# Grouped TensorE products in a two-layer hybrid encoder: chained units, fewer state copies, and attention values placed before the next transposes

## The chip, the cores and the metric

The kernel runs on one core of a Trainium2 chip. The metric is the time of one execution on the device in microseconds (us), as the median of several runs.

## What is computed

Two layers, each with three parallel branches on 256 tokens of width 1024, then a gated feed-forward block. All inputs and outputs are float32. Cut to what the change touches:

```python
for l in range(DEPTH):                      # DEPTH = 2
    h = _rmsnorm(x, norm1_g[l])
    # one projection h @ w_in[l], split into q, k, v, gate of the retention branch,
    # the low-rank inputs of attention, s5_u, and the three branch gates
    ...
def attend(blk):                            # attention branch, 8 heads, 256 keys
    sc = einsum('bhqd,bhkd->bhqk', qn, k_nope) + einsum('bhqd,bkd->bhqk', qr, k_rope)
    p = softmax(sc, axis=-1)
    return einsum('bhqk,bhkd->bhqd', p, v)
...
# S5 branch, both directions: 64 groups of 16 channels, a complex state of 64 each
bu = einsum('bsgc,gpc->bsgp', u_g, bb)      # re and im
x_t = abar * x_{t-1} + bu_t                 # associative scan over the 256 tokens
y = Re(einsum('bsgp,gcp->bsgc', x, c))      # + d * u, then gelu and a GLU
```

## The kernel before

**Main work.** Weights are streamed from HBM in tiles of 512 KB (`raw`). ScalarE rounds a tile to a high part (`wh`, L668), VectorE subtracts to get the low part (`wl`, L669), and TensorE makes three products for each block of 128 rows (`mm3`, L673 to L675: high by high, high by low, low by high) into the PSUM banks of pool `pw`. These products of 256 columns are called main products below. They run in both layers from start to end.

**S5 work.** The S5 branch is a generator (`s5`) that the main work advances in small steps (`tick`), so that its instructions are traced between the main products. The 256 tokens are cut into 32 blocks of 8. For each of 16 steps `qq` (four groups of 16 channels at a time) `s5_wt` builds weights on VectorE (L523 to L531), transposes them on TensorE (L536, four in a bank of `p5`) and copies them out (L538). Then four products, one for each group, go to four strips of 32 columns of the array (`tile_position`, L452, tile `p`, called state products). After every second step the bank is copied (L459), transposed (L462) and written by ScalarE in eight copies of 64 by 128 elements into the state tile `SS` (L467, L468). In layer 1 the built weights come back from HBM (`wtd`). After a scan over the blocks on VectorE (L480 to L483), `s5_out` makes for each step `q` a set of small kernels: two directions by four strips (L584, tile `p`), whose bank goes to HBM as `kd` and comes back in another layout as `wt`; `s5_emit` then accumulates the outputs of two steps (L629, tile `pa`, called output products): for each step the products with the forward states, with the backward states (both read `wy`) and with `wt`. A float32 product is two instructions on TensorE, a transpose is one.

**Attention.** `attend` (L1110 on) goes over eight heads: `score` (four products, L1134 and L1135, then maximum, exponent and scaling on VectorE and ScalarE), `turn` (four transposes, L1153, and one copy, L1156), and the product with the values (L1170, two for each head, two heads in one bank). Between them `more` pulls steps of the first branch's main products.

**What sets the order.** The program is traced and a scheduler then orders each engine's instructions by priority, by its own estimate of when operands and buffers are ready; every engine works through its list in order. PSUM has eight banks: three in `pw`, three in `pa` (scores, transposes, attention values, output products), two in `p5` (everything else of S5). Buffers of a tag rotate: a new tile waits until the readers of an old one are done. Two banks of `p5` mean that a second set of L536 transposes waits while a bank of transposed states is still read by the copies L467 and L468. SBUF buffers named `at` hold the scores and their transposes, two before the change.

## Time and profile before

| what | us |
|---|---|
| median of three runs | 1431.8 (1431.16 to 1436.98) |
| the profiled execution | 1425.45 |
| its span | 1423.5 |
| TensorE (PE) busy | 1334.4, 94% |
| VectorE (DVE) busy | 1042.3, 73% |
| ScalarE (ACT) busy | 807.0, 57% |

Busy times of PE are of pipelined instructions, whose shown durations overlap: a main product lasts 0.28 us in the records, and the next begins 0.12 us after it. What an instruction costs on PE is therefore read from start to start. The chain of work that ended last lies on PE for 68% of the span. S5 states are built between about 65 and 222 us in layer 0 and between 820 and 887 us in layer 1; S5 outputs between 298 and 443 us and between 976 and 1128 us, in the same stretches as attention.

### The profile page before, as it was taken

The page shows a single profiled execution, that of the slowest core. Times are in us where ns is not written, and L with a number is a line of the kernel's source. Part 1 is how long each engine was busy: PE and PEld are TensorE (multiplying, and loading weights), DVE is VectorE, ACT ScalarE, POOL GpSimd, SP SyncE. Part 2 cuts the span into 40 slices and gives each one's busy share as a digit, 9 for nine tenths or more (in the row PEclk, how much of TensorE's full clock was granted, in tenths as well). Part 3 has the DMA queues.
Part 4 walks back from the last instruction along what each step waited for, and adds up shares of the span by engine and source line. Part 5 has one row for each costly group of instructions (what it writes and reads, how often), then busy time and mean ns, then how long its engine had stood idle before and what let it go on. Part 6 is the DMA issues. An engine that isn't in the chain of part 4 may idle for free.

```text
span 1423.5 us, 27613 instructions
## 1 busy us (share of the span) xinstructions
PE 1334.4 (94%) x11102; PEld 1234.2 (87%) x11102; DVE 1042.3 (73%) x1910; ACT 807.0 (57%) x1339; POOL 4.5 (0%) x33
## 2 busy tenths in 40 slices
PE   7899998888999999999999999788999999999997
PEld 5866878867888999999999868778988899999997
DVE  7977867877687679988668547877768657777754
ACT  3656576974654455545446677786564344544442
POOL 0000000000000000000000000000000000000000
PEclk9999999999999999999999999999999999999999
DMA  8944233646786699766679784365687667666662
GB/s 218 250 146 118 69 104 99 182 137 152 211 219 194 201 211 260 210 199 197 188 229 273 239 267 131 99 193 156 157 247 188 193 200 204 181 185 187 179 179 79
DMA packets 433891, 260.84 MB, mean 183 GB/s; under 512 B 61714, under 2 KB 413284, under 8 KB 433764
## 3 DMA queue, kind: packets, MB, share of 16 engines
q1 hardware_dynamic: 433764, 259.09, 64.3%
q8 instruction: 87, 1.43, 0.4%
q14 instruction: 40, 0.33, 0.1%
HBM read 231.53 MB, written 27.53 MB: 182 GB/s over the span
## 4 chain that ended last, share of the span: by engine, by line
PE 68%; ACT 13%; DMA 8%; DVE 6%; issue 3%; SPq 1%; DVEq 0%; ACTq 0%
PE pw L673 17%; PE pw L674 17%; PE pw L675 17%; DMA wt<-kd 3%; ACT wh L668 3%; PE pw L713 2%; PE pw L714 2%; PE pw L715 2%; DVE wl L669 2%; DMA kd<-ev 2%; ACT s L497 2%; PE p L536 2%; PE p L452 2%; DMA raw<-in_w_in 1%; SPq L121 1%
## 5 line engine op out<-in xcount | busy, mean ns | idle before, releaser
L673 PE MATMUL pw<-s,wh 128*128 128x256 f32 x2472 | 714.6, 290 | 16.6 <-ACT wh L668 13.8
L675 PE MATMUL pw<-s,wl 128*128 128x256 f32 x2472 | 703.5, 285 | 8.4 <-DVE wl L669 8.3
L674 PE MATMUL pw<-s,wh 128*128 128x256 f32 x2472 | 703.0, 285 | 0.2 <-DVE s L749 0.2
L668 ACT CAST wh<-raw 128x1024 fp32r<-128x1024 f32 (+4 forms) x394 | 381.0, 972 | 456.2 <-PE pw L674 290.7
L669 DVE TENSOR_TENSOR wl<-raw,wh 128x1024 fp32r<-128x1024 f32 (+4 forms) x394 | 443.1, 1128 | 206.8 <-ACT wh L668 205.4
L673 PEld LDWEIGHTS pw<-s,wh 128*128 128x128 f32 x2472 | 472.1, 191 | 34.1 <-ACT wh L668 16.6
L675 PEld LDWEIGHTS pw<-s,wl 128*128 128x128 f32 x2472 | 472.5, 191 | 15.5 <-DVE wl L669 11.2
L674 PEld LDWEIGHTS pw<-s,wh 128*128 128x128 f32 x2472 | 472.9, 191 | 6.6 <-issue 4.8
L713 PE MATMUL pw<-s,wh 128*128 128x256 f32 x256 | 71.9, 281 | 0.0
L714 PE MATMUL pw<-s,wh 128*128 128x256 f32 x256 | 71.9, 281 | 0.0
L715 PE MATMUL pw<-s,wl 128*128 128x256 f32 x256 | 71.9, 281 | 0.0
L569 DVE TENSOR_TENSOR wy<-s,s 128x512 f32<-128x512 f32 x64 | 42.3, 687 | 16.1 <-PE pa L629 10.3
L715 PEld LDWEIGHTS pw<-s,wl 128*128 128x128 f32 x256 | 48.2, 188 | 0.0
L714 PEld LDWEIGHTS pw<-s,wh 128*128 128x128 f32 x256 | 48.2, 188 | 0.0
L713 PEld LDWEIGHTS pw<-s,wh 128*128 128x128 f32 x256 | 48.2, 188 | 0.0
L536 PE MATMUL p<-ident,wy 128*128 128x128 f32 x256 | 36.7, 276 | 11.5 <-ACT s L468 11.1
L497 ACT COPY s<-s 64x256 f32<-64x256 f32 (+1 forms) x64 | 40.7, 636 | 5.2 <-DVE s L483 4.3
L536 PEld LDWEIGHTS p<-ident,wy 128*128 128x128 f32 x256 | 28.6, 140 | 16.6 <-ACT s L468 13.2
L570 DVE TENSOR_TENSOR tm<-s,s 128x512 f32<-128x512 f32 x64 | 43.0, 687 | 0.0
L571 DVE TENSOR_TENSOR wy<-wy,tm 128x512 f32<-128x512 f32 x64 | 42.7, 685 | 0.0
L748 ACT ACTIVATE s<-ev 128x512 fp32r<-128x512 f32 x46 | 29.1, 633 | 19.7 <-DVE ev L1350 12.1
L531 DVE TENSOR_TENSOR wy<-wy,tm 128x1024 f32<-128x1024 f32 x32 | 39.1, 1221 | 0.3
(284 smaller groups left out, 1549.7 us busy)
## 6 DMA issues: line engine op xcount, KB each, us to landing
raw<-in_w_in SPq DMA_DIRECT2D x122, 512.0 KB
raw<-in_ffn_w_gu SPq DMA_DIRECT2D x88, 512.0 KB
raw<-in_w_branch SPq DMA_DIRECT2D x48, 512.0 KB
raw<-in_s_w_glu SPq DMA_DIRECT2D x32, 512.0 KB
raw<-in_ffn_w_down SPq DMA_DIRECT2D x32, 512.0 KB
wt<-kd SPq DMA_DIRECT2D x64, 128.0 KB
raw<-in_w_out SPq DMA_DIRECT2D x16, 512.0 KB
wtd<-wt SPq DMA_DIRECT2D x16, 512.0 KB
```

Source lines behind the costliest of these rows:

```text
L497: A.copy(*todo.pop(0))
L536: T.transpose(ps[:, i * P:(i + 1) * P], W[i % 2][:, gp * 2 + i // 2].rearrange("p s c -> p (s c)"), self.ident)
L570: V.tensor_tensor(t2, tv(1), cv(C2), ALU.mult)
L571: V.tensor_tensor(y[:, :, js, :], y[:, :, js, :], t2, ALU.add)
L668: self.nc.scalar.copy(hi, src)
L669: self.nc.vector.tensor_tensor(lo, src, hi.bitcast(F32), ALU.subtract)
L673: T.matmul(ps, lh, rh, start=first, stop=False)
L674: T.matmul(ps, lh, rl, start=False, stop=False)
L675: T.matmul(ps, ll, rh, start=False, stop=last)
L713: T.matmul(o, wh[:, k, c], xh, start=(half == 0 and m == 0 and k == 0), stop=(k == 3), **f)
L714: T.matmul(o, wh[:, k, c], xl, start=False, stop=(k == 3), **f)
L715: T.matmul(o, wl[:, k, c], xh, start=False, stop=(k == 3), **f)
```

## The change

A context manager `unit` is added: it records an ordering edge between each two PE instructions that are traced in it, from one to the one before, so that the scheduler keeps their order among themselves. It is put around the state products, the transposes L462 and L536, the kernels L584, and the products and transposes of retention and attention. Within such groups the order is changed so that those that need the operand that is made last come first.

The eight copies into `SS` become four of 64 by 256 elements. Before, a copy read runs of 32 neighbours in PSUM and wrote each element 256 bytes from the last; now it writes runs of eight neighbours and reads PSUM at steps of 128 bytes.

In `s5_emit` the products with the states of both steps come first, and then those with `wt` of both. In `attend` the value product of a head is put off until the transposes of the next head, after both calls of `more`; `more` counts to 17 instead of 16; `at` gets a third buffer, and the buffers of the scan (`sc`) go from four to two.

```diff
+    @contextmanager
+    def unit(self):
+
+        traced = self.nc.cur_bb.bb.instructions
+        n = len(traced)
+        yield
+        last = None
+        for i in traced[n:]:
+            if i.engine != mybir.EngineType.PE:
+                continue
+            if last is not None:
+                self.tc.add_manual_dep(i, last.name, mybir.DependencyInfo(
+                    mybir.DependencyClass.NoSync, mybir.DependencyReason.DATA), reason="unit")
+            last = i
...
-            for g4 in range(4):
-                T.matmul(plv[g4 * 32:g4 * 32 + 32, :],
-                         UT[qq // 8][:, qq % 8, g4 * 32:g4 * 32 + 32],
-                         WT[:, g4].rearrange("p r x -> p (r x)"), start=True, stop=True, tile_position=(0, g4 * 32))
+            with self.unit():
+                for g4 in (2, 3, 0, 1):
+                    T.matmul(plv[g4 * 32:g4 * 32 + 32, :],
+                             UT[qq // 8][:, qq % 8, g4 * 32:g4 * 32 + 32],
+                             WT[:, g4].rearrange("p r x -> p (r x)"), start=True, stop=True,
+                             tile_position=(0, g4 * 32))
...
-            for i in range(4):
-                T.transpose(pt[:, i * P:(i + 1) * P], lq[:, i * P:(i + 1) * P], self.ident)
-            ptv = pt.rearrange("p (q r h n) -> p q r h n", q=2, r=2, h=4)
-            for q2 in range(2):
-                g0 = (qq - 1 + q2) * 4
-                for r in range(2):
-                    A.copy(SS[0:64, r, :, g0:g0 + 4].rearrange("p n h -> p h n"), ptv[0:64, q2, r])
-                    A.copy(SS[64:128, r, ::-1, g0:g0 + 4].rearrange("p n h -> p h n"), ptv[64:128, q2, r])
+            with self.unit():
+                for i in range(4):
+                    T.transpose(pt[:, i * P:(i + 1) * P], lq[:, i * P:(i + 1) * P], self.ident)
+            ptv = pt.rearrange("p (q r h n) -> p r n q h", q=2, r=2, h=4)
+            g0 = (qq - 1) * 4
+            for r in range(2):
+                o = lambda rows, step: SS[rows, r, ::step, g0:g0 + 8].rearrange("p n (q h) -> p n q h", q=2)
+                A.copy(o(slice(0, 64), 1), ptv[0:64, r])
+                A.copy(o(slice(64, 128), -1), ptv[64:128, r])
...
-            r1 = self.s(128, "sc", 4).rearrange("p (r g) -> p r g", r=2)
-            r2 = self.s(128, "sc", 4).rearrange("p (r g) -> p r g", r=2)
+            r1 = self.s(128, "sc", 2).rearrange("p (r g) -> p r g", r=2)
+            r2 = self.s(128, "sc", 2).rearrange("p (r g) -> p r g", r=2)
...
-            for d in range(2):
-                for g4 in range(4):
-                    gm = q * 4 + g4
-                    c0 = (q % 2) * 240 + (112 if d == 0 else 0)
-                    js = slice(0, 8) if d == 0 else slice(1, 9)
-                    T.matmul(pk[g4 * 32:g4 * 32 + 32, c0:c0 + 128],
-                             BB2[:, d, gm * 16:gm * 16 + 32],
-                             Y[d][:, g4, js, :].rearrange("p j c -> p (j c)"),
-                             start=(d == 0), stop=True, tile_position=(0, g4 * 32), skip_group_check=(d == 1))
+            with self.unit():
+                for d in (1, 0):
+                    for g4 in range(4):
+                        gm = q * 4 + g4
+                        c0 = (q % 2) * 240 + (112 if d == 0 else 0)
+                        js = slice(0, 8) if d == 0 else slice(1, 9)
+                        T.matmul(pk[g4 * 32:g4 * 32 + 32, c0:c0 + 128],
+                                 BB2[:, d, gm * 16:gm * 16 + 32],
+                                 Y[d][:, g4, js, :].rearrange("p j c -> p (j c)"),
+                                 start=(d == 1), stop=True, tile_position=(0, g4 * 32), skip_group_check=(d == 0))
...
-        for q_, Yq in pend:
-            oc = (q_ % 4) * 128
-            for k in range(3):
-                for g4 in range(4):
-                    gm = q_ * 4 + g4
-                    if k == 0:
-                        lhsT, rhs = Sf[:, gm, :], Yq[0][:, g4, 1:9, :].rearrange("p j c -> p (j c)")
-                    elif k == 1:
-                        lhsT, rhs = Sb[:, gm, :], Yq[1][:, g4, 0:8, :].rearrange("p j c -> p (j c)")
-                    else:
-                        lhsT, rhs = UT[:, q_, g4 * 32:g4 * 32 + 32], M[:, g4, q_ % 2, :]
-                    T.matmul(po[g4 * 32:g4 * 32 + 32, oc:oc + 128], lhsT, rhs, start=(k == 0), stop=(k == 2),
-                             tile_position=(0, g4 * 32))
+        for ks in ((0, 1), (2,)):
+            for q_, Yq in pend:
+                oc = (q_ % 4) * 128
+                for k in ks:
+                    for g4 in range(4):
+                        gm = q_ * 4 + g4
+                        if k == 0:
+                            lhsT, rhs = Sf[:, gm, :], Yq[0][:, g4, 1:9, :].rearrange("p j c -> p (j c)")
+                        elif k == 1:
+                            lhsT, rhs = Sb[:, gm, :], Yq[1][:, g4, 0:8, :].rearrange("p j c -> p (j c)")
+                        else:
+                            lhsT, rhs = UT[:, q_, g4 * 32:g4 * 32 + 32], M[:, g4, q_ % 2, :]
+                        T.matmul(po[g4 * 32:g4 * 32 + 32, oc:oc + 128], lhsT, rhs,
+                                 start=(k == 0 and q_ % 2 == 0), stop=(k == 2), tile_position=(0, g4 * 32),
+                                 skip_group_check=True)
...
-            while done[1] < done[0] * steps // 16:
+            while done[1] < done[0] * steps // 17:
...
-            for kt in range(2):
-                for t in range(2):
-                    T.transpose(pt[:, kt * S + t * P:kt * S + t * P + P], pe[:, t * S + kt * P:t * S + kt * P + P],
-                                self.ident)
+            with self.unit():
+                for t in (1, 0):
+                    for kt in range(2):
+                        T.transpose(pt[:, kt * S + t * P:kt * S + t * P + P],
+                                    pe[:, t * S + kt * P:t * S + kt * P + P], self.ident)
             pts = self.s(512, "at")
             A.copy(pts, pt)
             return pts
 
-        pe = score(0)
-        for hd in range(MH):
-            more()
-            pts = turn(pe)
-            if hd + 1 < MH:
-                pe = score(hd + 1)
-            more()
+        def value(hd, pts):
             if hd % 2 == 0:
-                po = self.bank(self.pa)
-            vv, hh = kvs[hd // 4][1], hd % 4
+                value.po = self.bank(self.pa)
+            po, vv, hh = value.po, kvs[hd // 4][1], hd % 4
             for kt in range(2):
                 T.matmul(po[:, (hd % 2) * S:(hd % 2 + 1) * S], vv[:, kt * 512 + hh * MV:kt * 512 + (hh + 1) * MV],
                          pts[:, kt * S:(kt + 1) * S], start=(kt == 0), stop=(kt == 1))
             if hd % 2 == 1:
                 self.put(y, hd - 1, 2, po)
+
+        pe, held = score(0), None
+        for hd in range(MH):
+            more()
+            more()
+            if held:
+                value(hd - 1, held)
+            held = turn(pe)
+            if hd + 1 < MH:
+                pe = score(hd + 1)
+        more()
+        value(MH - 1, held)
         run(work)
```

Indentation apart, the other hunks put `with self.unit():` around loops that stay as they were; the transposes of retention's `finish` also change their order as those of `turn` do. A line of before and its number after the change: L452 is L469, L536 is L556, L629 is L651, L673 to L675 are L696 to L698, L1134 and L1135 are L1161 and L1162, L1153 is L1181, L1170 is L1192.

How the instructions stand on PE in layer 0, where states are built, from the second set of L536 transposes of a step (weights of step `qq` = 2) on. Before:

```order
L536 MATMUL p_171_905<-ident,wy_892 128x128 x4
L452 MATMUL p_172_911<-wt_898,s_124_625 32x256 x2
L673 MATMUL pw_922<-s_34_212,wh_925 128x256
L674 MATMUL pw_922<-s_36_214,wh_925 128x256
L675 MATMUL pw_922<-s_34_212,wl_926 128x256
L673 MATMUL pw_922<-s_34_212,wh_925 128x256
L452 MATMUL p_172_911<-wt_898,s_124_625 32x256 x2
```

The same place after the change:

```order
L556 MATMUL p_171_901<-ident,wy_888 128x128 x4
L697 MATMUL pw_918<-s_35_213,wh_921 128x256
L698 MATMUL pw_918<-s_33_211,wl_922 128x256
L696 MATMUL pw_918<-s_34_212,wh_921 128x256
L697 MATMUL pw_918<-s_36_214,wh_921 128x256
L698 MATMUL pw_918<-s_34_212,wl_922 128x256
L696 MATMUL pw_918<-s_34_212,wh_921 128x256
L697 MATMUL pw_918<-s_36_214,wh_921 128x256
L698 MATMUL pw_918<-s_34_212,wl_922 128x256
L469 MATMUL p_172_907<-wt_894,s_124_625 32x256 x4
```

The two halves of a step's state products, with four main products between them, have become one group behind eight main products.

PE in layer 1, the first output products (`s5_emit`) of that layer. Before:

```order
L629 MATMUL pa_11463<-wy_11410,s_1706_10257 32x128 x4
L629 MATMUL pa_11463<-wy_11410,s_1707_10258 32x128 x4
L629 MATMUL pa_11463<-wt_11609,s_1574_9529 32x128 x4
L629 MATMUL pa_11463<-wy_11520,s_1706_10257 32x128 x4
L629 MATMUL pa_11463<-wy_11520,s_1707_10258 32x128 x4
L629 MATMUL pa_11463<-wt_11609,s_1574_9529 32x128 x4
L1170 MATMUL pa_11751<-at_11625,s_1881_11099 128x256 x2
```

The same place after the change:

```order
L651 MATMUL pa_11396<-wy_11346,s_1706_10193 32x128 x4
L651 MATMUL pa_11396<-wy_11346,s_1707_10194 32x128 x4
L651 MATMUL pa_11396<-wy_11430,s_1706_10193 32x128 x4
L651 MATMUL pa_11396<-wy_11430,s_1707_10194 32x128 x4
L651 MATMUL pa_11396<-wt_11541,s_1574_9497 32x128 x8
L696 MATMUL pw_11626<-s_1422_8677,wh_11689 128x256
```

The products with `wt`, which comes from HBM, stand eight products later for the first of the two steps.

PE in layer 0, attention, transposes of the second head and scores of the third. Before, where two sets of S5 transposes (L389) lie among the scores:

```order
L675 MATMUL pw_3133<-s_244_1292,wl_3184 128x256
L1153 MATMUL pa_3273<-ident,at_3082 128x128 x4
L1134 MATMUL pa_3280<-s_552_2897,s_486_2615 128x256
L389 MATMUL p_627_3256<-ident,s_624_3249 128x128 x4
L1135 MATMUL pa_3280<-kab_2182,s_488_2617 128x256
L1134 MATMUL pa_3280<-s_552_2897,s_486_2615 128x256
L389 MATMUL p_628_3264<-ident,s_624_3249 128x128 x4
L1135 MATMUL pa_3280<-kab_2182,s_488_2617 128x256
```

The same place after the change, with the values of the first head ahead:

```order
L698 MATMUL pw_3241<-s_34_212,wl_3245 128x256
L1192 MATMUL pa_3293<-at_3082,s_553_2866 128x256 x2
L1181 MATMUL pa_3296<-ident,at_3094 128x128 x4
L1161 MATMUL pa_3303<-s_552_2865,s_486_2583 128x256
L1162 MATMUL pa_3303<-kab_2154,s_488_2585 128x256
L1161 MATMUL pa_3303<-s_552_2865,s_486_2583 128x256
L1162 MATMUL pa_3303<-kab_2154,s_488_2585 128x256
L696 MATMUL pw_3241<-s_33_211,wh_3321 128x256
```

Values, transposes and scores stand in a row here. In the whole program that is so for two heads of sixteen (one before); value products stand directly ahead of a set of transposes seven times (twice before).

In the whole program the state products stand in 30 runs of two, 15 of four and one of eight before, and in 30 of four and one of eight after; the kernels L584 in 20 runs of four and 22 of eight before, and in 31 of eight, one of five and one of three after. PE has 10076 products and transposes both times, ACT 66 instructions fewer.

## Rows read from the trace of the kernel before

**Rows 1.** The page's first part: busy us, share of span, instructions, by engine.

```profile
PE 1334.4 (94%) x11102; PEld 1234.2 (87%) x11102; DVE 1042.3 (73%) x1910; ACT 807.0 (57%) x1339; POOL 4.5 (0%) x33
```

**Rows 2.** Stretches: length, busy PE, PEld, DVE, ACT, POOL, clock, DMA share, GB/s.

```profile
75.00:215.00 140.00, 128.58 (x858) 102.55 (x857) 105.50 (x202) 86.95 (x158) 0.54 (x4) 0.98 0.36 104
450.00:800.00 350.00, 347.77 (x2874) 343.95 (x2873) 281.13 (x423) 182.84 (x252) 0.17 (x1) 1.00 0.77 218
```

**Rows 3.** PE's timeline: start us, us; a half and a full group of state products.

```profile
130.77 0.28 PE L674 MATMUL pw<-s,wh 128*128 128x256 f32 x1
130.89 0.28 PE L675 MATMUL pw<-s,wl 128*128 128x256 f32 x1
131.10 0.63 PE L452 MATMUL p<-wt,s 128*32 128x256 f32 x4
...
131.88 0.28 PE L674 MATMUL pw<-s,wh 128*128 128x256 f32 x1
...
872.29 0.28 PE L675 MATMUL pw<-s,wl 128*128 128x256 f32 x1
872.49 0.64 PE L452 MATMUL p<-wt,s 128*32 128x256 f32 x8
...
873.28 0.28 PE L674 MATMUL pw<-s,wh 128*128 128x256 f32 x1
```

**Rows 4.** PE's timeline: a half and a full group of the kernels L584.

```profile
402.68 0.28 PE L675 MATMUL pw<-s,wl 128*128 128x256 f32 x1
402.90 0.43 PE L584 MATMUL p<-wy,t_bb 128*32 128x128 f32 x8
...
403.48 0.28 PE L674 MATMUL pw<-s,wh 128*128 128x256 f32 x1
...
1086.17 0.28 PE L675 MATMUL pw<-s,wl 128*128 128x256 f32 x1
1086.38 0.64 PE L584 MATMUL p<-wy,t_bb 128*32 128x128 f32 x16
...
1087.18 0.28 PE L674 MATMUL pw<-s,wh 128*128 128x256 f32 x1
```

**Rows 5.** PE's waits from 75 to 215 us: total us, times, longest us.

```profile
PE p L536 <- ACT s L468: 11.1, 7, 1.8
```

**Rows 6.** ACT's copies by form: busy us, mean ns, idle before.

```profile
L497 ACT COPY s<-s 64x256 f32<-64x256 f32 x48 | 31.3, 652 | 5.0 <-DVE s L483 4.3
L467 ACT COPY s<-p 64x128 f32<-64x128 f32 x64 | 24.2, 378 | 2.1 <-PE p L462 1.5
L373 ACT COPY s<-ev 64x256 f32<-64x256 f32 x8 | 3.2, 406 | 1.1 <-DMA ev<-pxd 1.1
```

**Rows 7.** A wait for the copies on PE's timeline, and the stretch behind it.

```profile
82.07 0.66 PE L536 MATMUL p<-ident,wy 128*128 128x128 f32 x4 [1.74 <-ACT s L468]
...
83.00:86.40 3.40, 3.40 (x16) 1.98 (x13) 1.92 (x3) 1.40 (x3) 0.00 (x0) 0.50 0.38 134
```

**Rows 8.** Waits for `wt` (300 to 450, 975 to 1130 us); 48 output products in the chain.

```profile
PE pa L629 <- DMA wt<-kd: 7.8, 14, 1.1
...
PE pa L629 <- DMA wt<-kd: 3.6, 5, 1.0
...
399.42 1.45 PE pa L629 x48
```

**Rows 9.** DVE's largest wait from 75 to 215 us.

```profile
DVE wl L669 <- ACT wh L668: 14.5, 14, 5.1
```

**Rows 10.** Attention: PE's wait for a bank (300 to 450 us); ACT's copy; ACT's cast.

```profile
PE pa L1134 <- ACT at L1156: 0.9, 1, 0.9
...
L1156 ACT COPY at<-pa 128x512 f32<-128x512 f32 x16 | 9.4, 588 | 3.0 <-PE pa L1153 2.9
...
L668 ACT CAST wh<-raw 128x1024 fp32r<-128x1024 f32 (+4 forms) x394 | 381.0, 972 | 456.2 <-PE pw L674 290.7 <-issue 86.8 <-PE pw L714 35.0
```

More of the change, by code (lines that the diff above doesn't have):

```diff
@@ L1 @@
 import math
+from contextlib import contextmanager
 import numpy as np
@@ L935, in score @@
             qh, kh = q[:, hd * S:(hd + 1) * S], k[:, hd * S:(hd + 1) * S]
-            for s_ in range(2):
-                T.matmul(ps[:, s_ * S:(s_ + 1) * S], kh[:, s_ * P:(s_ + 1) * P], qh, start=True, stop=True)
+            with self.unit():
+                for s_ in range(2):
+                    T.matmul(ps[:, s_ * S:(s_ + 1) * S], kh[:, s_ * P:(s_ + 1) * P], qh, start=True, stop=True)
             V.scalar_tensor_tensor(dec, ps, sc, dec, ALU.mult, ALU.mult)
@@ L942, in value @@
             py = self.bank(self.pa)
-            for tt in range(2):
-                for s_ in range(2):
-                    T.matmul(py[:, tt * S:(tt + 1) * S], dec[:, s_ * S + tt * P:s_ * S + tt * P + P],
-                             vt[s_][:, hd * RV:(hd + 1) * RV], start=(s_ == 0), stop=(s_ == 1))
+            with self.unit():
+                for tt in range(2):
+                    for s_ in range(2):
+                        T.matmul(py[:, tt * S:(tt + 1) * S], dec[:, s_ * S + tt * P:s_ * S + tt * P + P],
+                                 vt[s_][:, hd * RV:(hd + 1) * RV], start=(s_ == 0), stop=(s_ == 1))
             st = self.s(12, "gst", 2).rearrange("p (t x) -> p t x", t=2)
@@ L964, in finish @@
             ps = self.bank(self.pa)
-            for i in range(2):
-                for tt in range(2):
-                    T.transpose(ps[:, i * S + tt * P:i * S + tt * P + P],
-                                yn[:, tt * S + i * P:tt * S + i * P + P], self.ident)
+            with self.unit():
+                for tt in (1, 0):
+                    for i in range(2):
+                        T.transpose(ps[:, i * S + tt * P:i * S + tt * P + P],
+                                    yn[:, tt * S + i * P:tt * S + i * P + P], self.ident)
             for i in range(2):
```

20 lines of the change are left out of this document (11 added, 9 removed).

## The prediction

> **What bounds the kernel now.** I read the busy times first [rows 1]: TensorE is busy for 94% of the span, VectorE for 73%, ScalarE for 57%. So time can be saved in two ways only: PE needs less time for the same products, or PE waits less. Then the stretches [rows 2]. From 450 to 800 us, where main products alone run, PE is never late although VectorE is busy for 80% (281.1 of 350 us). From 75 to 215 us, where S5 states are built, PE is busy for 92% (128.6 of 140 us) and VectorE for 75%. The change acts in the second kind of stretch. Last, PE's timeline start to start, because busy times of pipelined products overlap: this shows what a group of strip products costs in its place.
>
> **State products, L452.** A half group (two products, four instructions) stands between two main products. From the main product ahead of it to the second one behind it are 0.99 us (130.89 to 131.88), and a full group of eight instructions takes the same 0.99 us (872.29 to 873.28) [rows 3]. Two strips cost as much as four: the time goes into the passes that the strips share, and into entering and leaving. Both stretches hold two main products, at 0.12 us each (130.77 to 130.89) [rows 3]. Two halves cost 2 x 0.99 = 1.98 us; one full group and the two main products that then stand elsewhere cost 0.99 + 0.24 = 1.23 us. Each joining saves 0.75 us, and the order shows 15 (30 runs of two become 15 of four): 11.2 us, nearly all in the stretch from 75 to 215 us.
>
> **Kernels, L584.** A half group takes 0.80 us (402.68 to 403.48), a full one 1.01 us (1086.17 to 1087.18) [rows 4]; here the strips are full anyway and only entering and leaving is saved. Joining saves 2 x 0.80 - 1.01 - 0.24 = 0.35 us. The order goes from 42 runs to 33: 9 x 0.35 = 3.2 us. The runs of output products go from 31 to 30, which I leave out. PE time saved: 14.4 us. It lies on the path as far as PE is the bound there.
>
> **Copies into the state tile.** In layer 0 PE waits seven times for them, 11.1 us in all, before the second set of L536 transposes [rows 5]: both banks of `p5` are taken, one by the transposed states until the eighth copy has read them. Eight copies at 0.38 us make 3.04 us [rows 6]. What one of the four new copies takes, no row shows. Lower end: 0.41 us, a copy of 64 by 256 without scattered access (L373). Upper end: 0.76 us, the old price for each element. The nearest row in shape is L497 with 0.65 us: it also writes runs of eight and reads at wide steps, but from SBUF [rows 6]. The source here is PSUM, so I take 0.53 us, midway between L373 and L497. Four copies make 2.12 us; each of the seven waits shrinks by 0.92 us, as ten main products or so still stand ahead of the waiting transposes: 6.4 us. The ends are 7 x (3.04 - 1.64) = 9.8 us and nothing. Layer 1's eight sets and layer 0's last relieve ScalarE alone, counted at nothing.
> [...]
>
> **The clock.** [...] I take 0.8 us; ends 0 and 3 us, for another such place.
>
> **Output products, L629.** PE waits 19 times for `wt` from HBM, 7.8 + 3.6 = 11.4 us [rows 8]. Up to four of these waits belong to one call of `s5_emit`, so 5 to 16 calls wait. Now the second step's products with the states, 16 instructions, come first: 48 take 1.45 us [rows 8], so 0.48 us of work moves ahead of the wait. I take seven calls: 3.4 us; ends 2.4 and 7.7 us. The DMAs behind it are the same and stand at the same places on SP's queue relative to the kernels that feed them.
>
> **Attention.** The value products now come after more main products, so their copy is ready; that can only help PE. Scores follow the transposes as before, in 10 heads instead of 12 without main products between them. PE waited for a bank there once, 0.9 us [rows 10]. I put the sum at nothing; ends a gain of 2 us and the loss of the fourth rival. `at` with three buffers and `sc` with two: each step of the scan needs the step before it, so two `sc` buffers hide nothing, and cost nothing.
>
> **What is given back.** With 11.2 + 6.4 + 0.8 = 18.4 us less, the stretch of 140 us would be 121.6 us long, and VectorE's 105.5 us there would be 87% of it, above the 80% that another stretch bears without waits [rows 2]. VectorE also waits 14.5 us for ScalarE's casts there [rows 9], and these waits don't vanish all. To come down to 80% the stretch needs 131.9 us, which gives 10.3 us back. I take 4 us, nearer to nothing, because the buffers for high and low parts let VectorE work ahead; ends 0 and 10.3 us.
>
> **The sum.** 14.4 + 6.4 + 0.8 + 3.4 - 4 = 21.0 us less. The profiled execution took 1425.45 us (span 1423.5 and about 2 us around it), so it would take 1404.4 us. The runs' median is 1431.8, 6.4 us above the profiled execution, and I put the difference on the median: 1410.8, so 1411 us. All good ends: 14.4 + 9.8 + 3 + 7.7 + 2 = 36.9 us less, 1395 us. All bad ends short of a loss: 14.4 + 0 + 0 + 2.4 - 10.3 = 6.5 us less, 1425 us.
>
> **Rivals.**
> First, VectorE becomes the bound where states are built: waits of main products for low parts (L675 for L669) take the place of those for the copies. For it: 87% by the sum. Against it: 80% without waits elsewhere. Given back are 10 us and more of the 18.4; with 10.3 instead of 4 the time is 1417 us, and if the whole stretch gains nothing, 3.2 + 3.4 = 6.6 us less remain, 1425 us. Chance 0.16.
> Second, the units are not kept together as meant. The order speaks against it for the strips, where the counts above are from the changed program; for attention it is half so (two heads of sixteen wholly in a row), and that part has no term in the sum. Time as forecast; no chance of its own.
> Third, the new copies cost 0.76 us each: seven waits of the old length, no clock gain. The stretch is then 128.8 us long and VectorE at 82%, so 1 us is given back: 14.4 + 3.4 - 1 = 16.8 us less, 1415 us. [...] Chance 0.13.
> Fourth, slower: banks of `pa` in attention. While S5 outputs are made, one of three banks holds the output products and one the values, now until the head's end. Transposes and next scores share the third, and scores wait for the copy: 0.59 us, with a cast of 0.97 us ahead of it on ScalarE, and where a pair of values has just been put out another copy of 0.59 us [rows 10]: up to 2.15 us. Behind the scores on PE the main products wait. At sixteen heads that is 34 us, 13 us more than the gain: 1445 us. From 1.3 us for each head the gain is gone. Against it: the one wait of 0.9 us in the old order, which has the same neighbourhood of transposes and scores. Chance 0.07.
>
> **How the numbers follow.** The forecast, 1411 us give or take 8, has 0.64, the rivals 0.16, 0.13 and 0.07. The range from 1395 to 1425 us takes in the forecast with its ends and the first and third rival, and leaves the fourth out, and a tenth for what I don't see. A measurement of this kernel can tell about 0.5% from no change, 7 us: faster means under 1424.6 us. The forecast and the third rival lie there nearly whole, the first for the larger part: 0.83. The same: 0.10, the rest of the first and mishaps. Slower: 0.07.
>
> **What would show it.** L452 in groups of eight instructions in layer 0, from main product to main product 0.99 us; L584 in sixteens; the wait of L536's successor for the copies from 11.1 us to about 5 us; the new copies near 0.5 us; waits for `wt` from 11.4 to about 8 us; VectorE over 80% from 75 us to the end of the state building, with short waits of L675's successor for low parts. Wrong it would be if the joined groups wait for their last operand longer than a half group cost, if copies take 0.76 us, or if scores wait over 1 us for a bank.

## The result and the profile after

The changed kernel takes 1396.4 us, median of four runs (1395.9 to 1396.9), against 1432.6 us before (1431.2 to 1437.0). The ratio is 0.9755, with a 95% interval of 0.9734 to 0.9776. The forecast was 1411 us, faster; the time lies in the range of 1395 to 1425 us, at its good end, and outside the 8 us around the forecast. The profiled execution took 1396.14 us with a span of 1394.1 us. From trace to trace that is 29.3 us less, from median to median 36.2 us. The two differ because the profiled execution of before (1425.45 us) is quicker than every timed run of that kernel. What lies in between is told at the clock, below.

Busy time by engine, first part of the page of the changed kernel, beside [rows 1]:

```profile
PE 1323.2 (95%) x11102; PEld 1236.3 (89%) x11102; DVE 1041.3 (75%) x1910; ACT 779.3 (56%) x1273; POOL 4.6 (0%) x33
```

PE is busy for 11.2 us less with as many instructions, ACT for 27.7 us less with 66 fewer. The span has shrunk by 29.4 us, so 18.2 us of the gain, well over half, is time in which PE stood idle.

PE's timeline of the changed kernel (start us, us, group, and in brackets the idle time ahead of it), first a group of state products in layer 0, then a group of the kernels; beside [rows 3, 4]:

```profile
122.16 0.28 PE L696 MATMUL pw<-s,wh 128*128 128x256 f32 x1
122.39 0.64 PE L469 MATMUL p<-wt,s 128*32 128x256 f32 x8
122.96 0.39 PE L697 MATMUL pw<-s,wh 128*128 128x256 f32 x1
123.18 0.28 PE L698 MATMUL pw<-s,wl 128*128 128x256 f32 x1
```

```profile
301.29 0.28 PE L697 MATMUL pw<-s,wh 128*128 128x256 f32 x1
301.50 0.64 PE L605 MATMUL p<-wy,t_bb 128*32 128x128 f32 x16
302.07 0.39 PE L698 MATMUL pw<-s,wl 128*128 128x256 f32 x1
302.29 0.28 PE L696 MATMUL pw<-s,wh 128*128 128x256 f32 x1
```

The state products stand in eights in layer 0 now. From the main product ahead to the second one behind are 1.02 us (122.16 to 123.18), where a half group had taken 0.99 us. The kernels stand in sixteens at 1.00 us.

ACT's new copies into the state tile, by form (busy us, mean ns, idle before), and PE's wait for them in layer 0 (total us, times, longest); beside [rows 5, 6]:

```profile
L487 ACT COPY s<-p 64x256 f32<-64x256 f32 x32 | 11.8, 367 | 0.4
L486 ACT COPY s<-p 64x256 f32<-64x256 f32 x32 | 11.6, 363 | 1.3 <-PE p L481 1.1
```

```profile
PE p L556 <- ACT s L487: 2.0, 6, 0.4
```

A copy of twice the elements takes 0.365 us, less than the old one with 0.379 us. PE's waits fall from 11.1 us to 2.0 us. The place behind the old wait of 1.74 us [rows 7], in PE's timeline and as a stretch (length, busy PE, PEld, DVE, ACT, POOL, clock, DMA share, GB/s), with the whole stretch of the state building under it:

```profile
82.40 0.66 PE L556 MATMUL p<-ident,wy 128*128 128x128 f32 x4 [0.38 <-ACT s L487]
```

```profile
82.80:86.20 3.40, 3.19 (x31) 2.58 (x30) 2.29 (x4) 2.38 (x5) 0.00 (x0) 1.00 0.76 223
75.00:205.00 130.00, 127.13 (x946) 107.89 (x945) 113.96 (x224) 84.08 (x147) 0.65 (x4) 1.00 0.44 124
```

The wait is 0.38 us now and the granted clock stays at 1.00: 31 PE instructions start in 3.4 us, where 16 did at 0.50. In two experiments below waits of 1.73 and 1.76 us at this place leave the clock at 1.00. PE is busy for 98% of the stretch. VectorE is busy for 88% of it (113.96 of 130 us), and yet no wait for its low parts is on PE's list there. Its own wait for ScalarE's casts in that stretch fell from 14.5 us [rows 9] to this:

```profile
DVE wl L692 <- ACT wh L691: 5.5, 9, 1.0
```

PE's waits for `wt` (285 to 450 us, 960 to 1130 us), beside [rows 8], and its waits in attention for the copy of the transposes, beside [rows 10]:

```profile
PE pa L651 <- DMA wt<-kd: 5.1, 8, 0.9
PE pa L1161 <- ACT at L1184: 1.0, 1, 1.0
...
PE pa L651 <- DMA wt<-kd: 4.0, 7, 1.0
```

```profile
PE pa L1192 <- ACT at L1184: 3.4, 1, 3.4
```

The waits for `wt` went from 11.4 us to 9.1 us. Scores wait once for a bank, 1.0 us. One new wait of 3.4 us is there: in layer 1 a pair of value products waits for its copy. Before the change, transposes in that stretch (880 to 980 us there) had waited 2.4 us for ScalarE.

### The profile page after: what moved, and what is told of

Its sections match the earlier page's. It is cut to its first block, busy times and chain, and to the rows that moved or that the text cites. A ratio compares the mean times of both kernels' runs of the same rounds, so it can differ in the third digit from the quotient of the medians.

```text
span 1394.1 us, 27529 instructions
## 1 busy us (share of the span) xinstructions
PE 1323.2 (95%) x11102; PEld 1236.3 (89%) x11102; DVE 1041.3 (75%) x1910; ACT 779.3 (56%) x1273; POOL 4.6 (0%) x33
## 4 chain that ended last, share of the span: by engine, by line
PE 69%; ACT 9%; DVE 6%; DMA 6%; issue 2%; SPq 1%; DVEq 0%; ACTq 0%
PE pw L696 18%; PE pw L697 17%; PE pw L698 17%; DMA wt<-kd 3%; ACT wh L691 2%; PE pw L737 2%; PE pw L738 2%; PE pw L736 2%; DVE wl L692 2%; ACT s L516 2%; DMA kd<-ev 2%; PE p L556 2%; SPq L122 1%; PE p L469 1%; PE pa L651 1%
## 5 line engine op out<-in xcount | busy, mean ns | idle before, releaser
L696 PE MATMUL pw<-s,wh 128*128 128x256 f32 x2472 | 715.1, 290 | 13.1 <-ACT wh L691 10.1
L698 PE MATMUL pw<-s,wl 128*128 128x256 f32 x2472 | 703.2, 285 | 5.8 <-DVE wl L692 5.6
L691 ACT CAST wh<-raw 128x1024 fp32r<-128x1024 f32 (+3 forms) x394 | 380.9, 972 | 451.9 <-PE pw L697 290.5
L692 DVE TENSOR_TENSOR wl<-raw,wh 128x1024 fp32r<-128x1024 f32 (+3 forms) x394 | 442.6, 1127 | 215.4 <-ACT wh L691 200.2
L696 PEld LDWEIGHTS pw<-s,wh 128*128 128x128 f32 x2472 | 473.5, 192 | 28.4 <-ACT wh L691 13.7
L698 PEld LDWEIGHTS pw<-s,wl 128*128 128x128 f32 x2472 | 473.4, 192 | 12.2 <-DVE wl L692 8.5
L589 DVE TENSOR_TENSOR wy<-s,s 128x512 f32<-128x512 f32 x64 | 42.6, 685 | 17.8 <-PE pa L651 11.4
L516 ACT COPY s<-s 64x256 f32<-64x256 f32 (+1 forms) x64 | 40.6, 635 | 4.2 <-DVE s L502 3.4
L696 PE MATMUL pw<-wh,s 128*128 128x512 f32 (+1 forms) x96 | 36.4, 381 | 4.2 <-ACT s L1124 4.2
L556 PE MATMUL p<-ident,wy 128*128 128x128 f32 x256 | 36.9, 276 | 2.4 <-ACT s L487 2.0
```

What stands on the lines that cost most here:

```text
L516: A.copy(*todo.pop(0))
L556: T.transpose(ps[:, i * P:(i + 1) * P], W[i % 2][:, gp * 2 + i // 2].rearrange("p s c -> p (s c)"), self.ident)
L691: self.nc.scalar.copy(hi, src)
L692: self.nc.vector.tensor_tensor(lo, src, hi.bitcast(F32), ALU.subtract)
L696: T.matmul(ps, lh, rh, start=first, stop=False)
L698: T.matmul(ps, ll, rh, start=False, stop=last)
```

## The experiments

Most start from the changed kernel and take one part back, or from the kernel before and do one part alone; the last two go on from the changed kernel. In a table first; before has a median of 1432 us in each of the three series. The differences in the last column are between medians of four to six runs, and the changed kernel was timed in a series of its own; no interval was worked out for them. Runs of one of these kernels lie 3 to 9 us apart, so a difference of 1 to 3 us can't be told from nothing.

| kernel | median us (runs) | against before, 95% | against the changed kernel |
|---|---|---|---|
| changed | 1396.4 (1395.9 to 1396.9) | 0.9734 to 0.9776 | |
| eight copies again | 1410.4 (1407.8 to 1412.3) | 0.9816 to 0.9866 | +14.0 |
| four copies, scattered writes | 1406.2 (1402.3 to 1407.7) | 0.9774 to 0.9838 | +9.8 |
| states split again | 1407.5 (1405.0 to 1408.4) | 0.9797 to 0.9843 | +11.1 |
| kernels split again | 1399.3 (1396.4 to 1401.8) | 0.9732 to 0.9788 | +2.8 |
| output products by step again | 1399.3 (1395.7 to 1404.3) | 0.9734 to 0.9794 | +2.9 |
| attention's order of before | 1397.6 (1396.1 to 1398.9) | 0.9724 to 0.9778 | +1.2 |
| copies alone | 1413.7 (1408.9 to 1420.1) | 0.9820 to 0.9908 | |
| states alone | 1421.4 (1413.0 to 1422.5) | 0.9871 to 0.9942 | |
| copies and states | 1406.7 (1402.8 to 1410.2) | 0.9795 to 0.9856 | |
| attention alone | 1427.3 (1424.8 to 1428.4) | 0.9956 to 0.9982 | |
| GpSimd takes half of L516 | 1383.7 (1381.9 to 1386.0) | 0.9633 to 0.9694 | -12.8 |
| L516 in the other order | 1396.0 (1394.0 to 1401.2) | 0.9727 to 0.9788 | -0.4 |

**State products taken apart again.**

```diff
-            with self.unit():
-                for g4 in (2, 3, 0, 1):
-                    T.matmul(plv[g4 * 32:g4 * 32 + 32, :],
+            for g4 in range(4):
+                T.matmul(plv[g4 * 32:g4 * 32 + 32, :],
```

> The changed kernel with the four state products of a step not held together and in strip order 0, 1, 2, 3 as before; all else as changed. Theory A (a half-filled group costs what a full one does, 0.75 us for each of 15 joinings): 11 us above the changed kernel, near 1408, and TensorE's groups of two in layer 0 cost 0.75 us more than they hold. Theory B (the time came back as waits elsewhere, since VectorE is 87% busy there): 3 us or less above it, and the waits for the low parts (L698 for wl) shrink by what the products take longer.

It is 11.1 us slower. PE's timeline of this kernel shows two halves in layer 0, with four main products between them:

```profile
75.53 0.62 PE L468 MATMUL p<-wt,s 128*32 128x256 f32 x4
76.09 0.39 PE L694 MATMUL pw<-s,wh 128*128 128x256 f32 x1
...
76.56 0.28 PE L694 MATMUL pw<-s,wh 128*128 128x256 f32 x1
76.77 0.63 PE L468 MATMUL p<-wt,s 128*32 128x256 f32 x4
77.32 0.39 PE L695 MATMUL pw<-s,wh 128*128 128x256 f32 x1
77.55 0.28 PE L696 MATMUL pw<-s,wl 128*128 128x256 f32 x1
```

The half group takes 0.99 us (76.56 to 77.55), nearly as much as the whole one above. Theory A holds: half a group costs nearly what a group does, and PE's list of waits for this kernel (75 to 215 us) has none for low parts. VectorE was not the bound.

**State products alone, on the kernel before.** The same lines, the other way round.

> The kernel before with only the state products of a step held together, in strip order 2, 3, 0, 1. Theory A: 11 us faster, near 1421, the waits for the copies (11 us at L536) stay as they are. Theory B (fewer products of the gate between two transposes, so PE comes to the bank sooner and waits longer): the wait at L536 grows to 15 us or more and the gain is below 6 us.

It is 10.7 us faster, and PE's wait for the copies is the old one:

```profile
PE p L554 <- ACT s L486: 11.1, 7, 1.8
```

So by the medians the joining has its price on its own, whether the copies are there or not: 10.7 us alone and 11.1 us taken out. Theory B, a longer wait behind fewer products, falls: the wait is unchanged. The profiled execution shows only 2.9 us (1422.51 against 1425.45 us), at a mean granted clock of 0.979 against 0.982. Its state building is shorter by 14.5 us (table below). Behind it the same work, some 9840 PE instructions, took 1212.1 us against 1203.2 us, with PE busy 8.4 us longer: one trace beside another can be off by that much.

**Eight copies again.**

```diff
-            ptv = pt.rearrange("p (q r h n) -> p r n q h", q=2, r=2, h=4)
+            ptv = pt.rearrange("p (q r h n) -> p q r h n", q=2, r=2, h=4)
...
+                    A.copy(SS[0:64, r, :, g0:g0 + 4].rearrange("p n h -> p h n"), ptv[0:64, q2, r])
```

> The changed kernel with the eight copies into SS of the kernel before in place of the four; all else as changed. Theory A (the copies hold the bank for the transposes behind them; four copies took 0.36 us each in the trace after, eight took 0.38 before): L556 (L536 before) waits for ACT about 11 us again in place of 2.0, ACT is busy 25 us more, and the time is 8 to 12 us above the changed kernel, near 1406. Theory B (the joined state products alone fill the gaps, the copies lie beside other work): within 3 us of the changed kernel, and the waits at L556 stay below 4 us.

It is 14.0 us slower, more than either theory. The waits at the transposes of layer 0, in this kernel's list, came back whole:

```profile
PE p L556 <- ACT s L487: 11.0, 7, 1.8
```

That is 9.0 us more than after. The rest is in layer 1, where no such transposes stand. There PE waits at the transposes of the products (L481, L462 before) for ScalarE's copy of them into `ev`. From the lists of PE's waits in layer 1 (825 to 995, 800 to 960 and 810 to 976 us) of the three kernels, before, changed, and this one, the row of that wait and the one for low parts:

```profile
PE pw L675 <- DVE wl L669: 5.4, 5, 3.1
...
PE p L462 <- ACT ev L459: 3.0, 3, 1.3
```

```profile
PE pw L698 <- DVE wl L692: 3.6, 4, 1.5
...
PE p L481 <- ACT ev L477: 0.4, 1, 0.4
```

```profile
PE pw L698 <- DVE wl L692: 6.1, 5, 3.0
PE p L481 <- ACT ev L477: 3.6, 3, 1.3
```

The `ev` copy stands on ScalarE behind the copies of the pair before; in the trace of before a cast stands between them in five of seven places. The state products of layer 1 run, in the same order of kernels, from first to last start:

```profile
L452 PE MATMUL p<-wt,s x128: 379/379/403, 820.6 to 872.8; 128*32 128x256 f32 x128
```

```profile
L469 PE MATMUL p<-wt,s x128: 376/379/403, 794.5 to 843.8; 128*32 128x256 f32 x128
```

```profile
L469 PE MATMUL p<-wt,s x128: 376/379/403, 805.3 to 857.7; 128*32 128x256 f32 x128
```

52.2, 49.3 and 52.4 us: 3 us in layer 1 belong to the copies, as much as that wait. Behind it PE's waits for low parts (L698) are 6.1 us in place of 3.6 us, which need casts that stand on ScalarE behind its copies too. 9.0 + 3.1 + 2.5 us make 14.6 us of the 15.3 us between the two traces.

**Copies alone, on the kernel before.**

> The kernel before with only the four copies into SS in place of the eight. Theory A (waits for the bank, and the clock behind them): the wait of L536 for ACT falls from 11.1 to about 2 us and the time by 8 to 12 us, to 1421 to 1424. Theory B (the copies bring their gain only with the joined state products, since the split ones let other work between): less than 4 us.

PE's wait is the short one:

```profile
PE p L536 <- ACT s L468: 2.0, 6, 0.4
```

The runs lie from 1408.9 us at a mean granted clock of 0.986 to 1420.1 us at 0.977. By the medians the copies bring 18.4 us, by the profiled execution 9.5 us (1425.45 to 1415.97, at 0.982 and 0.981). Theory A has the wait right, and the time by the trace only: the medians lie beyond its 8 to 12 us. How much the copies bring alone stays open between 9.5 and 18.4 us, since time and clock vary together from run to run.

**Four copies that write in steps.** The number stays at four; the order of the elements is the old one.

```diff
-            ptv = pt.rearrange("p (q r h n) -> p r n q h", q=2, r=2, h=4)
+            ptv = pt.rearrange("p (q r h n) -> p r q h n", q=2, r=2, h=4)
...
-                o = lambda rows, step: SS[rows, r, ::step, g0:g0 + 8].rearrange("p n (q h) -> p n q h", q=2)
+                o = lambda rows, step: SS[rows, r, ::step, g0:g0 + 8].rearrange("p n (q h) -> p q h n", q=2)
```

> The changed kernel with four copies that take the same elements in the order of the old ones: they read the bank in runs and write SS with steps of 64 elements. Theory A (the write at wide steps sets the price: 64x128 took 0.378 us before, so twice as much takes 0.62 to 0.76): the copies take 0.6 us or more, and the time is 3 to 8 us above the changed kernel. Theory B (the number of copies alone matters): 0.36 us each, and no difference above 1 us.

Its copies by form, and PE's wait:

```profile
L487 ACT COPY s<-p 64x256 f32<-64x256 f32 x32 | 19.4, 606 | 0.4
L486 ACT COPY s<-p 64x256 f32<-64x256 f32 x32 | 19.2, 602 | 1.2 <-PE p L481 1.0
```

```profile
PE p L556 <- ACT s L487: 8.6, 7, 1.3
```

0.604 us in place of 0.365 us: the copies are where theory A had them. The time lost, 9.8 us by the medians and 6.1 us by the profiled executions, is at or above the upper end of its 3 to 8 us. What made the new copies cheap is the order in which they write, runs of eight elements. That they read the bank in steps costs nothing here (0.365 us): a plain copy of 256 elements out of PSUM took as long (0.364 us), in the trace of before,

```profile
L1026 ACT COPY ev<-pw 32x256 f32<-32x256 f32 x8 | 2.9, 364 | 0.1
```

Fewer instructions alone would have brought PE's wait from 11.1 to 8.6 us only.

**Kernels taken apart again, output products by step again.**

```diff
-            with self.unit():
-                for d in (1, 0):
-                    for g4 in range(4):
+            for d in range(2):
+                for g4 in range(4):
```

> The changed kernel with the kernels L605 (L584 before) not held together and in the order d = 0, 1 of before. Theory A (0.35 us for each of 9 joinings): 3 us above the changed kernel. Theory B (nothing: what is split here is filled with products of the gate at no price): within 1 us.

```diff
-        for ks in ((0, 1), (2,)):
-            for q_, Yq in pend:
-                oc = (q_ % 4) * 128
-                for k in ks:
+        for q_, Yq in pend:
+            oc = (q_ % 4) * 128
+            for k in range(3):
```

> The changed kernel with the output products step by step as before, so that the products with wt of a first step stand ahead of the second step's own. Theory A (wt comes from HBM and is waited for): the waits of L629 for wt go from 9.1 us in the trace after to 11 to 13, and the time is 2 to 4 us above the changed kernel. Theory B (the wait only moves to another load): within 1 us.

Both medians, 2.8 and 2.9 us above the changed kernel, are where theory A had them. But each has a run at the changed kernel's time (1396.4 and 1395.7 us), and for the kernels the two profiled executions differ by 0.2 us. A gain between nothing and 3 us is what the first shows. For the second the profiled executions differ by 3.3 us, and the waits have moved the expected way, but not to 11 us or more:

```profile
PE pa L650 <- DMA wt<-kd: 10.0, 17, 1.0
```

10.0 us against 9.1 us after: 0.9 us of the 3 us are seen at these waits.

**The attention.** The changed kernel with the head's order of before (shown in part), and the kernel before with the new order (there the scan's buffers `sc` go to two as well).

```diff
         for hd in range(MH):
             more()
-            more()
-            if held:
-                value(hd - 1, held)
-            held = turn(pe)
+            pts = turn(pe)
             if hd + 1 < MH:
                 pe = score(hd + 1)
+            more()
```

> The changed kernel with the attention heads in the order of before: a share of other work, transposes, next scores, another share, values; scores and transposes of a head still held together. Theory A (my sum: the attention's part is worth nothing, between a gain of 2 us and a loss): within 3 us of the changed kernel. Theory B (the order of the heads is what brought the 6 to 8 us that the timed runs show beyond the sum of the other parts): 5 us or more above it.

> The kernel before with only the attention of the changed one: values one head later and directly ahead of the transposes, transposes and scores of a head held together, a third buffer for the transposed weights. Theory A (worth 1 us, as taking the order back out of the changed kernel cost): within 4 us of the kernel before. Theory B (it earns more where the S5 work around it is not regrouped): 5 us or more faster.

In the changed kernel the order is worth 1.2 us, which the runs can't tell from nothing. The waits for `wt` are moved by it more than by the order in `s5_emit`: with the old order of the heads they are 13.5 us in the whole program, against 9.1 us after. On the kernel before it is worth 4.7 us by the medians, with an interval of 2.6 to 6.3 us. The profiled executions don't show it (1426.12 us at a clock of 0.985, and 1425.45 us at 0.982). The runs of that kernel have granted clocks from 0.981 to 0.986, those of before beside it from 0.976 to 0.984. The clock could account for the 4.7 us, but the profiled execution has the higher clock without the gain, so the cause is open.

**Copies and states together.**

> The kernel before with both the four copies and the joined state products, and nothing else. Theory A (the two add: 14 to 18 for the copies and 11 for the products, as they measured alone and taken out): 25 to 29 us faster, 1403 to 1407, and the clock of its runs at 0.983 or more. Theory B (they want the same gaps): 20 us faster or less.

25.3 us faster, the lower end of theory A; alone the two have 18.4 and 10.7 us, so nearly all adds up. Its clock is 0.978 to 0.983, below that of the changed kernel and of what theory A expected: 1402.8 us at 0.983, 1410.2 us at 0.978.

The stage where both parts act can be compared without the rest of the program: in each trace, the time from the first to the last start of a state product in layer 0, with the granted clock from 75 to 200 us.

| kernel | us (from, to) | clock |
|---|---|---|
| before | 152.8 (67.4, 220.2) | 0.97 |
| copies alone | 139.2 (71.2, 210.4) | 1.00 |
| states alone | 138.3 (70.0, 208.3) | 1.00 |
| copies and states | 128.8 (70.8, 199.6) | 1.00 |
| changed | 129.0 (70.7, 199.7) | 1.00 |
| eight copies again | 138.8 (69.4, 208.2) | 1.00 |
| states split again | 139.3 (71.1, 210.4) | 1.00 |

Taken out of the changed kernel, the copies are worth 9.8 us here and the joined states 10.3 us. The whole stage is 23.8 us shorter, so 3.7 us are left, and either part alone already has them. They go with the clock: before ran slowly in two places there, behind waits for the copies of 1.74 us (to 82.07; clock 0.50 from 83.0 to 86.4 us) and 1.68 us (to 102.27; clock 0.69 from 102.2 to 105.6 us). But such a wait wasn't enough to bring the clock down. The kernel with only the states joined has one of 1.73 us at the same place, and what follows runs at a clock of 1.00:

```profile
83.24 0.66 PE L554 MATMUL p<-ident,wy 128*128 128x128 f32 x4 [1.73 <-ACT s L486]
...
84.00:87.40 3.40, 3.19 (x31) 2.57 (x30) 1.76 (x3) 2.61 (x4) 0.00 (x0) 1.00 0.50 151
```

The kernel with eight copies again has a wait of 1.76 us there and keeps its clock of 1.00 too. Of the kernels in the table only the one with both the waits and the split states ran slowly: before, at 0.97. What brings the clock down is open.

**GpSimd takes half of the copies out of the state tile.** After the scan's steps ScalarE copies the states out (L516), 64 copies in both layers. Each second one goes to GpSimd.

```diff
                 if todo:
-                    A.copy(*todo.pop(0))
+                    (nc.gpsimd.tensor_copy if len(todo) % 2 else A.copy)(*todo.pop(0))
```

> The changed kernel with half of the copies out of SS (L516, 0.65 us each on ACT) on GpSimd, which is busy 4.6 us in all. Theory A (ACT's queue is what the casts L691 and with them TensorE wait for at the end of the state building, 6.2 us from 205 to 280): the casts come sooner, 3 to 6 us below the changed kernel, near 1392. Theory B (GpSimd and VectorE slow each other while the state steps L502 run on VectorE, or GpSimd's copies take several times as long): 2 to 15 us above it.

1383.7 us, 12.8 us below the changed kernel and the fastest of all. The copies by form on both engines, and one of the four VectorE instructions of a step of the scan, in this kernel:

```profile
L516 POOL COPY s<-s 64x256 f32<-64x256 f32 x24 | 20.2, 841 | 173.8 <-DVE s L502 173.0
L516 ACT COPY s<-s 64x256 f32<-64x256 f32 x24 | 15.6, 650 | 4.1 <-DVE s L502 3.8
...
L501 DVE TENSOR_TENSOR sc<-sc,s 128x128 f32<-128x128 f32 x62 | 20.7, 334 | 0.0
```

and that instruction and PE's wait for the casts from 190 to 300 us in the changed kernel:

```profile
L501 DVE TENSOR_TENSOR sc<-sc,s 128x128 f32<-128x128 f32 x62 | 17.6, 284 | 0.0
```

```profile
PE pw L696 <- ACT wh L691: 6.2, 3, 2.4
```

and here:

```profile
PE pw L696 <- ACT wh L691: 2.4, 2, 1.7
```

Theory B's slowing is there, 50 ns for this instruction (284 to 334 ns), some 10 us of VectorE's time in all, beside 20.2 us that GpSimd's 24 copies of that form take. The kernel is faster all the same: what PE waited for in that stretch was ScalarE's casts, 6.2 us in the changed kernel and 2.4 us here. Theory A has the direction right and less than half of the size. The larger part is in layer 1. The stretch behind its state products holds 749 PE instructions in the changed kernel and 747 here (length, busy PE, PEld, DVE, ACT, POOL, clock, DMA share, GB/s):

```profile
845.00:960.00 115.00, 100.41 (x749) 93.48 (x749) 94.35 (x264) 88.20 (x168) 0.00 (x0) 0.94 0.52 146
```

```profile
842.00:950.00 108.00, 97.69 (x747) 91.72 (x747) 99.09 (x263) 77.98 (x152) 12.02 (x16) 0.95 0.55 153
```

7 us less. PE's waits for low parts in these stretches fall from 3.6 to 0.8 us, and the wait of 3.4 us for the values' copy is gone. ScalarE's work falls from 88.2 to 78.0 us. Its queue is what PE waits for where states are finished: the edit takes work from ScalarE alone.

**The same copies in the other order.** They read in runs of 32 elements and write in steps of 32.

```diff
-                        todo.append((Sf[qh][rows, :, n0 + 1:n1 + 1],
-                                     SS[0:64, r, n0:n1, gs].rearrange("p n g -> p g n")))
+                        todo.append((Sf[qh][rows, :, n0 + 1:n1 + 1].rearrange("p g n -> p n g"),
+                                     SS[0:64, r, n0:n1, gs]))
```

> The changed kernel with the copies out of SS (L516) taking the same elements in the other order: they read SS in runs of 32 elements and write with steps of 32 elements, where they now read with steps of 64 and write runs of 8. Theory A (a step in the write and a step in the read of the same memory cost alike): 0.60 to 0.65 us each, as now, and the time within 2 us of the changed kernel. Theory B (only the stepped read is dear): 0.37 us each, ACT 17 us less busy, and the time 2 to 6 us below it.

```profile
L516 ACT COPY s<-s 64x256 f32<-64x256 f32 x48 | 31.4, 655 | 4.0 <-DVE s L502 3.4
```

655 ns against 652 ns [rows 6], and the time of the changed kernel: theory A. For these copies on ScalarE, within SBUF, a step on the read side (256 bytes) costs what a step on the write side (128 bytes) does.

## Why the forecast was right, and where its sum was off

The direction and the two mechanisms, joined strips and cheaper copies, are what the experiments show. The sum came to 21.0 us; the parts taken out one by one are worth 11.1 + 2.8 + 14.0 + 2.9 + 1.2 = 32.0 us, and the whole 36.2 us. The 4.2 us between are open: the units around the transposes L462 and L536 and in retention were never taken out. That all good ends together, 36.9 us, come near the 36.2 us is luck: the copies went beyond theirs, and the output products stayed far below.

- **State products**: forecast 11.2 us; 11.1 us taken out, 10.7 us alone, 10.3 us in the stage itself. The reading of the timeline start to start, half group against whole group, gave the price almost exactly. By busy times (0.63 and 0.64 us in [rows 3]) a joining would have come to 0.62 us in place of 0.75 us.
- **Kernels**: forecast 3.2 us; 2.8 us by the medians, 0.2 us by the profiled executions.
- **Copies and the clock behind them**: forecast 6.4 + 0.8 us; 14.0 us taken out. This is the step that failed, by half, and for three reasons. The copy was priced midway between two rows with their source in SBUF, at 0.53 us, and took 0.365 us, below even the lower end of 0.41 us; so the waits fell by 9.1 us. "What one of the four new copies takes, no row shows" overlooked a row of before: L1026, a copy of 256 elements out of PSUM at 0.364 us. "Layer 1's eight sets ... relieve ScalarE alone, counted at nothing" was wrong: the trace of before had the wait of L462 for `ev`, 3.0 us, and waits for low parts behind it, which end on the same queue. That wait doesn't name the copies but the copy that stands behind them on ScalarE, and the sum left it out. And the clock was taken from a single place, where there were two in that stage: 3.7 us go with it, near the upper end of 3 us. No run shows the 0.8 us. Behind the wait of 1.74 us PE began 16 instructions in 3.4 us at a clock of 0.50, and after the change 31 in as long at 1.00; the 15 fewer are, at the later pace, an estimated 1.6 us.
- **The clock**: the profiled execution has a mean granted clock of 0.982 before and 0.985 after. The timed runs have 0.976 to 0.984 before and 0.985 to 0.987 after. In the runs of before time and clock go together: 1427.4 us at 0.984, 1439.8 us at 0.977. The changed kernel's four runs lie within 1 us. A difference of 0.006 on 1430 us is 8.6 us of full-speed time, an upper estimate of what the clock gives in the timed runs, against 4.3 us between the two traces (0.003 of 1424 us). "I put the difference on the median" therefore carried 6.4 us over that the changed kernel doesn't have. The third rival's "seven waits of the old length, no clock gain" took the wait for the cause; with the states joined alone a wait of 1.73 us at the same place left the clock at 1.00. What drops the clock in which run is open: the timed runs leave no trace.
- **Output products**: forecast 3.4 us, the waits fell by 2.3 us, and 2.9 us came back when the part was taken out, with runs on both sides. But only 0.9 us of the waits came back with it, and the order of the heads moves them by 4.4 us. That the size is near is in part luck, and the way to it is not shown.
- **Attention**: forecast nothing, ends a gain of 2 us and a loss; 1.2 us in the changed kernel. Alone it had 4.7 us, more than the upper end. "Their copy is ready" failed at one place, the new wait of 3.4 us.
- **What is given back**: forecast 4 us; none was found. The busy share came out as worked out (87% forecast, 88% measured), but no wait of a main product for low parts followed. VectorE's idle time in that stretch had been a wait for ScalarE's casts, 14.5 us before and 5.5 us after. It was not the lighter ScalarE that took it away: with the copies alone it is 11.2 us (75 to 215 us), with the states alone 6.2 us. The casts themselves wait for PE, 23.2 us at one line (L674) of before from 65 to 222 us, so a faster PE calls for them sooner; that this is the reason is argued, not shown. With GpSimd VectorE got 10 us more to do and the kernel 12.8 us faster. A busy share was read as a limit, where the idle rest was a wait for others.

Of the rivals, the first (VectorE becomes the bound) is ruled out by the split states, which lost all of their 11 us, and by the missing waits for low parts. The third (0.76 us for a copy) is ruled out by the row: 0.365 us. These copies take each element of the bank from another place and yet took as long as L1026, which reads neighbours (0.364 us). On the side of SBUF the order did count: single elements written in steps took 0.604 us, runs of eight 0.365 us. The second was not tested; it had no price. The fourth (scores wait for a bank) came to one wait of 1.0 us.

The sum with the measured sizes, against the profiled executions: 11 for the states, 0.2 to 3 for the kernels, 14.6 for the copies, 0.9 to 3.3 for the output products make 27 to 32 us, and 29.3 us is what they differ by.

## What to carry to other kernels

Price a copy by the way it touches SBUF on either side, and turn it so that what it scatters is the PSUM side (here 0.365 us, against 0.604 us with the steps in SBUF); then follow its engine's queue to everything that stands behind it, in each stage, and not only to the wait that names the copy. Where strips of one PE pass are filled in two rounds, hold them together: here half a pass cost nearly a whole one (0.99 against 1.02 us). A busy share of 88% was no bound here, where the idle rest was a wait for somebody else, and a queue that others wait for may be worth lightening even onto a slower engine (here 12.8 us, with copies of 0.841 us on GpSimd against 0.650 us on ScalarE).

## What was not expected of the hardware

- ScalarE copied 64 by 256 elements from PSUM, read in steps, into runs of eight in SBUF in 0.365 us, as quick as a plain copy of 256 elements out of PSUM (0.364 us) and quicker than 0.406 us for an unscattered copy from SBUF to SBUF [rows 6]. With single elements written in steps it took 0.604 us, with steps on the read side in SBUF 0.652 us, with steps of 32 on the write side 0.655 us.
- GpSimd did such a copy within SBUF in 0.841 us, nearly a third longer than ScalarE's 0.650 us, and VectorE's steps beside it took 0.334 in place of 0.284 us.
- A wait of PE of 1.7 us was followed by 3.4 us at half the clock in one kernel (0.50), and by none in another with the same wait at the same place (1.00, states joined).
- Time and granted clock went together from run to run: before took 1427.4 us at 0.984 and 1439.8 us at 0.977. The changed kernel's four runs lie within 1 us, but that it is steadier is not shown: with L516 in the other order, at the same median, four runs lie 7 us apart.
